# A state space stage whose decays get buffers of their own and whose four groups run as one strand

## The chip, the cores and the metric

The kernel runs on one core of a Trainium2 chip. The metric is device time in microseconds of one execution. The engines are named as the profile names them: PE (matmul; PEld its weight loads), DVE, ACT, POOL, and SP, whose queue issues the DMAs.

## The reference

A diffusion backbone of two layers over 256 latent and 256 context tokens, model width 1024. Each layer projects the normalised tokens once, for a state space mixer that runs in both directions, a differential attention and two gates, merges both branches, and ends in a gated feed-forward part. The change lies in the mixer: 16 heads of 64 in 4 groups, state 128, chunks of 128 tokens.

```python
def ssd_scan(xs, dt, a_head, b_mat, c_mat, h0):
    xd = (xs * dt[..., None]).reshape(bsz, nc, SSD_CHUNK, g, r, p)
    a = (dt * a_head).reshape(bsz, nc, SSD_CHUNK, g, r).transpose(0, 3, 4, 1, 2)
    a_cs = jnp.cumsum(a, axis=-1)
    ...
    cb = jnp.einsum('bclgn,bcsgn->bgcls', cc, bc)
    decay_in = jnp.exp(segsum(a))
    y_diag = jnp.einsum('bgcls,bgrcls,bcsgrp->bclgrp', cb, decay_in, xd)
    ...
    states = jnp.einsum('bclgn,bgrcl,bclgrp->bcgrpn', bc, decay_to_end, xd)
    ...
    y_off = jnp.einsum('bclgn,bcgrpn,bgrcl->bclgrp', cc, h_in, jnp.exp(a_cs))
    y = (y_diag + y_off).reshape(bsz, n, n_heads, p)
```

It is done for latent and context tokens, forward and on flipped sequences, and both results are added. The last layer needs the mixer's output for latent tokens alone.

## The kernel before

Everything lies with channels on partitions and tokens along the free dimension, in tiles of 128 tokens: four in layer 0 (`NT = 4`), two in layer 1. Each large product takes its weight from a list, `plan`: a DMA of 512 KB into `raw` (L304, on SP), a cast to the high part `whi` on ACT (L313), the low part `wlo` on DVE (L314), and then three matmuls per block of weight (L407 to L409). Products write PSUM banks; those of tag "mm" are two in number, those of tag "s", for small results, three.

The state space stage of a layer runs through four groups `g`. For each, a product gives two `xs` tiles, which `xbc_evac` takes out of PSUM by a convolution over tokens: `chv` on ACT (L568), two steps on DVE (L571, L572), a tanh `cth` (L665) and `xs` on DVE (L666). Then two generators are queued in two `lanes`: `states(g)` in lane 0 and `outputs(g)` in lane 1. A product calls `pump()` after each block of its weight, which lets the first generator of either lane go on to its next `yield`. So the program order of the mixer's instructions is woven into that of the large products by the number of `yield`s; a scheduler then orders each engine's queue, and keeps the matmuls of `pmm` and `ptr` in program order. A third queue, `trickle`, advanced by `drip()`, reads modulation weights (`mraw`, L463) and multiplies them (`pmmod`, L465).

`states(g)` transposes `xs` into `xT` (L910) and BF into `bT` (L916), and does six steps of the state: `xd = xT * ddt` on POOL (L925), a matmul into `psstate`, and `h` on ACT (L933) or DVE (L935, L938). It sets `sh["done"]`.

`outputs(g)` does, tile by tile:
- `fetch(t)` (L952): a DMA on SP's queue that spreads a row of cumulated decays over 128 partitions into `cs`, both directions and four heads, 512 KB. The tag `cs` has two buffers.
- `head(t)`: the matmul `cb` and its masked copy `cbm` (L961, DVE); `cc = exp(cs)` (L966, ACT); one subtraction for each direction, in place, on POOL (L969); the minimum of the two directions (L972, DVE), written into the first half of `cs`; its exponential `E` into the second half (L974, ACT); `cc` times CF (L975, DVE).
- X: for each of four heads a copy on ACT (L991) and a step on DVE (L992), then X times `E` (L993, DVE).
- the matmuls `pyyd` of X with `xT` and of `cc` with the states `h`, which wait for `sh["done"]`; after the last tile `xs` is updated from the result (L1014).

```python
            raw = fetch(0)
            yield 1
            nxt = head(0, raw)
            if NT > 1:
                raw = fetch(1)
            yield 1
            for t in range(NT):
                ...
                if t + 1 < NT:
                    nxt = head(t + 1, raw)
                    yield 1
                if t + 2 < NT:
                    raw = fetch(t + 2)
```

Of the kernel before, what the change touches and what calls it, by code (L numbers as in the profile page):

```python
# [10 lines left out]
F32 = mybir.dt.float32  # L11
F32R = mybir.dt.float32r
AF = mybir.ActivationFunctionType
ALU = mybir.AluOpType
AX = mybir.AxisListType

P = 128
D = 1024
# [41 lines left out]
def hybrid_backbone_kernel(  # L60
# [7 lines left out]
    V, A, G, T = nc.vector, nc.scalar, nc.gpsimd, nc.tensor  # L68
# [7 lines left out]
    def nm(s):  # L76
        cnt[0] += 1
        return f"{s}_{cnt[0]}"

    def bank(tag, what=""):  # L80
        return psp.tile([P, 512], F32, tag=tag, name=nm("p" + tag + what), bufs={"mm": 2, "s": 3, "y": 2, "m": 1}[tag])
# [246 lines left out]
    lanes = ([], [])  # L328
# [246 lines left out]
    for i in range(DEPTH):  # L575
        if i:
            L = col[i]
            m = L["mod"]
        full = i < DEPTH - 1
        NT = 4 if full else 2  # L580
        N = NT * P
# [359 lines left out]
                yield 1  # L941
            sh["done"] = True

        def outputs(g, sh):
            while "xT" not in sh:
                yield None
            xT, h_in = sh["xT"], sh["h"]
            yb = [bank("y", "yd"), bank("y", "yd")]

            def fetch(t):  # L950
                cs = up.tile([P, 2, 4, P], F32, tag="cs", name=nm("cs"), bufs=2)
                nc.sync.dma_start(cs.rearrange("p d h l -> p d (h l)"),  # L952
                                  csd[t, :, 4 * g:4 * g + 4, :].rearrange("d h l -> d (h l)").partition_broadcast(P))
                return cs

            def head(t, cs):
                tsl = slice(t * P, (t + 1) * P)
                cb = bank("s", "cb")
                pmm(cb[:, 0:P], BF[g][:, tsl], CF[g][:, tsl], start=True, stop=True)
                cbm = up.tile([P, 2, P], F32, tag="cbm", name=nm("cbm"), bufs=2)  # L960
                V.tensor_tensor(cbm, cb[:, 0:P].unsqueeze(1).to_broadcast([P, 2, P]), tri2, op=ALU.mult)  # L961

                cc = up.tile([P, 2, 4, P], F32, tag="cc", name=nm("cc"), bufs=2)
                dirs = [dr for dr in range(2) if not (dr == 0 and t == 2) and not (dr == 1 and t == 3)]
                d0, d1 = dirs[0], dirs[-1] + 1
                A.activation(cc[:, d0:d1], cs[:, d0:d1], AF.Exp)  # L966

                for dr in range(2):
                    G.tensor_tensor(cs[:, dr], cs[:, dr],  # L969
                                    csc[:, t, 16 * dr + 4 * g:16 * dr + 4 * g + 4].unsqueeze(2).to_broadcast([P, 4, P]),  # L970
                                    op=ALU.subtract)
                V.tensor_tensor(cs[:, 0], cs[:, 0], cs[:, 1], op=ALU.min)  # L972
                E = cs[:, 1]
                A.activation(E, cs[:, 0], AF.Exp)  # L974
                V.tensor_tensor(cc[:, d0:d1].rearrange("p d h l -> p (d h) l"), cc[:, d0:d1].rearrange("p d h l -> p (d h) l"),  # L975
                                CF[g][:, tsl].unsqueeze(1).to_broadcast([P, 4 * (d1 - d0), P]), op=ALU.mult)
                return cbm, cc, E, dirs

            raw = fetch(0)
            yield 1  # L980
            nxt = head(0, raw)
            if NT > 1:
                raw = fetch(1)
            yield 1
            for t in range(NT):
                tsl = slice(t * P, (t + 1) * P)
                cbm, cc, E, dirs = nxt
                X = up.tile([P, 4, P], F32, tag="X", name=nm("X"), bufs=2)
# [3 lines left out]
                    V.scalar_tensor_tensor(X[:, h, :], cbm[:, 1, :], dcol[1], X[:, h, :], op0=ALU.mult, op1=ALU.add)  # L992
                V.tensor_tensor(X, X, E, op=ALU.mult)  # L993
                yield 1
                if t + 1 < NT:
                    nxt = head(t + 1, raw)
                    yield 1
                if t + 2 < NT:
                    raw = fetch(t + 2)
                while "done" not in sh:  # L1000
                    yield None
                for f in range(2):
                    for h in (2 * f, 2 * f + 1):
                        r = slice(64 * (h % 2), 64 * (h % 2) + 64)
                        pmm(yb[f][r, tsl], xT[:, t, h * 64:(h + 1) * 64], X[:, h, :], start=True, stop=False)
                    for dr in dirs:
                        for h in (2 * f, 2 * f + 1):
                            r = slice(64 * (h % 2), 64 * (h % 2) + 64)
                            pmm(yb[f][r, tsl], h_in[dr, t][:, h * 64:(h + 1) * 64], cc[:, dr, h, :],
                                start=False, stop=dr == dirs[-1])  # L1010
                yield 1
            for f in range(2):
                j = 2 * g + f
                V.scalar_tensor_tensor(xs[j][:, 0:N], xs[j][:, 0:N], L["D"][:, j:j + 1], yb[f][:, 0:N],  # L1014
                                       op0=ALU.mult, op1=ALU.add)
            done.append(g)
            yield 1

        for g in range(4):
            for f, o in enumerate(gemm_f(hh, hl, 512, KD)):  # L1020
                xbc_evac(o, 512, xs[2 * g + f], 2 * g + f)
            sh = {}
            lanes[0].append(states(g, sh))
            lanes[1].append(outputs(g, sh))

        def gate_s(p):
            for f, o in enumerate(gemm_f(hh, hl, N, KD)):
# [179 lines left out]
```

## Time and profile before

| | us |
|---|---|
| median of 3 runs | 1745.26 (1743.87 to 1746.32) |
| the profiled execution's own time | 1740.01 |
| its span | 1738.2, mean granted clock of PE 0.993 |
| PE, DVE, ACT, POOL busy | 1667.1, 1148.0, 848.2, 181.3 |

The stage of layer 0 lies from about 405 to 580 us of the span, that of layer 1 from about 1346 to 1480. Rows of the profile are read like this. A group of the page is: line, engine, operation, result <- operands, shape, xcount | busy us, mean ns of one | idle us of the engine just before, and what ended it. A group of DMAs ends in its size and the us from issue to landing. A row of the timeline is: start us, us from first start to last end, engine, line, operation, xcount, and in brackets the idle time before it and what released it. A row of waits is: what waited for what, us in total, times, longest. A row of a window is: the stretch, its length, busy us of each engine (and instructions), the clock that PE was granted (1.00 is 2.4 GHz, 0.50 is 1.2 GHz), the DMA engines' busy share and GB/s.

### The profile page before, as it was taken

How to read it: one execution, taken by the hardware profiler on the slowest of the kernel's cores; microseconds unless marked ns; L12 is line 12 of the kernel's file. 1: busy time of each engine (PE TensorE's matmuls, PEld its weight loads, DVE VectorE, ACT ScalarE, POOL GpSimd, SP SyncE). 2: the span in 40 equal slices, each digit the busy share in tenths (PEclk: the TensorE clock that was granted, in tenths of full speed). 3: DMA queues.
4: the chain of work that ended last, by engine and by line, in shares of the span. 5: the costliest groups of instructions: out<-in, count | busy, mean ns of one | idle time of the engine just before them, and what ended most of it. 6: DMA issues, size and time to landing. Idle time of an engine off the chain costs nothing. (4 is left out here: it accounts for less than half of the span.)

```text
span 1738.2 us, 27022 instructions
## 1 busy us (share of the span) xinstructions
PE 1667.1 (96%) x10547; PEld 1406.2 (81%) x10547; DVE 1148.0 (66%) x2008; ACT 848.2 (49%) x1567; POOL 181.3 (10%) x212
## 2 busy tenths in 40 slices
PE   7999999999988999999999999999999898989997
PEld 4788878777766788888888888788879788989997
DVE  4776667325988855766666326666675789779964
ACT  3565665413545423644444225555655455466653
POOL 3000010001433000300000002100000252010000
PEclk9999999999999999999999999999999999989999
DMA  9644333555443234233323335844535445646653
GB/s 317 215 127 126 115 119 108 166 173 146 121 107 100 74 109 146 74 97 97 97 87 95 92 108 161 255 146 146 152 93 171 121 110 144 199 154 185 193 176 117
DMA packets 233199, 240.71 MB, mean 138 GB/s; under 512 B 10908, under 2 KB 223551, under 8 KB 233071
## 3 DMA queue, kind: packets, MB, share of 16 engines
q1 hardware_dynamic: 230720, 237.14, 45.4%
q8 instruction: 83, 1.36, 0.3%
q0 software_dynamic: 1312, 1.03, 0.2%
q10 hardware_dynamic: 1039, 0.81, 0.1%
q14 instruction: 45, 0.37, 0.1%
HBM read 234.62 MB, written 4.33 MB: 137 GB/s over the span
## 5 line engine op out<-in xcount | busy, mean ns | idle before, releaser
L314 DVE TENSOR_TENSOR wlo<-raw,whi 128x1024 fp32r<-128x1024 f32 (+1 forms) x318 | 388.3, 1221 | 255.7 <-ACT whi L313 254.8
L313 ACT CAST whi<-raw 128x1024 fp32r<-128x1024 f32 (+1 forms) x318 | 329.2, 1036 | 378.4 <-PE pmmmm L408 146.6
L407 PE MATMUL pmmmm<-th,whi 128*128 128x512 f32 x744 | 306.3, 412 | 1.6 <-DVE chv L572 1.6
L408 PE MATMUL pmmmm<-tl,whi 128*128 128x512 f32 x744 | 296.5, 399 | 0.0
L409 PE MATMUL pmmmm<-th,wlo 128*128 128x512 f32 x744 | 295.6, 397 | 0.0
L407 PEld LDWEIGHTS pmmmm<-th,whi 128*128 128x128 f32 x744 | 140.5, 189 | 42.2 <-issue 7.9
L409 PEld LDWEIGHTS pmmmm<-th,wlo 128*128 128x128 f32 x744 | 140.4, 189 | 34.5 <-issue 1.0
L408 PEld LDWEIGHTS pmmmm<-tl,whi 128*128 128x128 f32 x744 | 140.5, 189 | 31.0 <-issue 2.2
L393 PE MATMUL pmmmm<-th,whi 128*128 128x256 f32 x480 | 138.5, 289 | 1.5 <-ACT whi L313 1.3
L395 PE MATMUL pmmmm<-th,wlo 128*128 128x256 f32 x480 | 134.7, 281 | 0.6 <-DVE wlo L314 0.6
L394 PE MATMUL pmmmm<-tl,whi 128*128 128x256 f32 x480 | 134.8, 281 | 0.0
L969 POOL TENSOR_TENSOR cs<-cs,csc 128x512 f32<-128x512 f32 x48 | 69.1, 1454 | 264.0 <-DMA cs<-csd 141.5
L393 PEld LDWEIGHTS pmmmm<-th,whi 128*128 128x128 f32 x480 | 90.7, 189 | 6.2 <-issue 3.8
L394 PEld LDWEIGHTS pmmmm<-tl,whi 128*128 128x128 f32 x480 | 90.8, 189 | 0.7 <-issue 0.4
L395 PEld LDWEIGHTS pmmmm<-th,wlo 128*128 128x128 f32 x480 | 90.6, 189 | 0.8 <-DVE wlo L314 0.8
L409 PE MATMUL psmm<-th,wlo 128*128 128x512 f32 x200 | 79.3, 397 | 0.0
L725 ACT ACTIVATE e<-psscore,nmx 128x512 f32<-128x512 f32 (+1 forms) x96 | 58.1, 610 | 43.5 <-DVE nmx L722 40.5
L408 PE MATMUL psmm<-tl,whi 128*128 128x512 f32 x200 | 79.2, 396 | 0.0
L521 POOL TENSOR_TENSOR rs<-ms,mhalf 128x2 f32<-128x2 f32 x9 | 6.3, 699 | 698.5 <-DVE ms L518 698.5
L407 PE MATMUL psmm<-th,whi 128*128 128x512 f32 x200 | 79.0, 395 | 0.0
L722 DVE TENSOR_REDUCE nmx<-psscore 128x1 f32<-128x512 f32 (+1 forms) x80 | 51.8, 684 | 34.3 <-PE psscore L85 34.2
L441 PE MATMUL pmmmm<-whi,th 128*128 128x256 f32 x256 | 74.3, 290 | 0.0
(346 smaller groups left out, 3899.0 us busy)
## 6 DMA issues: line engine op xcount, KB each, us to landing
raw<-in_w_in_dram SPq DMA_DIRECT2D x124, 512.0 KB, 4.0
raw<-in_w_up_dram SPq DMA_DIRECT2D x88, 512.0 KB, 3.6
mraw<-in_w_mod_dram SPq DMA_DIRECT2D x80, 512.0 KB, 4.7
raw<-in_w_down_dram SPq DMA_DIRECT2D x45, 512.0 KB, 3.6
cs<-csd SPq DMA_DIRECT2D x24, 512.0 KB, 5.8
boot<-in_w_mod_dram SPq DMA_DIRECT2D x16, 512.0 KB, 9.3
raw<-in_w_br_att_dram SPq DMA_DIRECT2D x16, 512.0 KB, 3.6
raw<-in_w_br_ssd_dram SPq DMA_DIRECT2D x16, 512.0 KB, 3.5
```

The source lines that it names most:

```text
L313: pin(A.copy(hi[:, 0:n, :], raw[:, 0:n, :]))
L314: pin(V.tensor_tensor(lo[:, 0:n, :], raw[:, 0:n, :], hi[:, 0:n, :].bitcast(F32), op=ALU.subtract))
L393: T.matmul(o[f], whi[:, kk, cs], xh, start=first, stop=False)
L394: T.matmul(o[f], whi[:, kk, cs], xl, start=False, stop=False)
L395: T.matmul(o[f], wlo[:, kk, cs], xh, start=False, stop=last)
L407: T.matmul(o, whi[:, k % 4, cs], hi[k][:, 0:n], start=k == 0, stop=False)
L408: T.matmul(o, whi[:, k % 4, cs], lo[k][:, 0:n], start=False, stop=False)
L409: T.matmul(o, wlo[:, k % 4, cs], hi[k][:, 0:n], start=False, stop=k == k_tiles - 1)
L441: T.matmul(b[:, n, :], hi[k][:, ts], whi[:, k % 4, :], start=k == 0 and n == 0, stop=False)
L722: V.tensor_reduce(nmx[:, cc, 0:ng], sc[cc].rearrange("p (g k) -> p g k", g=ng), axis=AX.X, op=ALU.max, negate=True)
L725: A.activation(e[cc][:, g * w:(g + 1) * w], sc[cc][:, g * w:(g + 1) * w], AF.Exp, bias=nmx[:, cc, g:g + 1], accum_out=sm[:, cc, g:g + 1])
L969: G.tensor_tensor(cs[:, dr], cs[:, dr], csc[:, t, 16 * dr + 4 * g:16 * dr + 4 * g + 4].unsqueeze(2).to_broadcast([P, 4, P]), op=ALU.subtract)
```

## The change

Three things, all in `outputs`:
- The minimum is written into a tile of its own, `E` (two buffers), and its exponential is taken in place there; `cs` is read for the last time by that minimum.
- The four generators `outputs(g)` become one, over 4 x NT items (group, tile). It is queued before group 0's product; heads and X of an item need neither `xs` nor the states, and what waits for `done` of the item's group are the matmuls of y alone. The `yield` after the head and the one before it become one; the one after a group's update of `xs` joins that of the last tile.
- Two fetches are issued at the start, a third after the first head, and item n + 3's after the head of item n + 1. `cs` keeps two buffers.

```diff
@@ -941,19 +941,19 @@
                 yield 1
             sh["done"] = True
 
-        def outputs(g, sh):
-            while "xT" not in sh:
-                yield None
-            xT, h_in = sh["xT"], sh["h"]
-            yb = [bank("y", "yd"), bank("y", "yd")]
-
-            def fetch(t):
+        shs = []
+
+        def outputs():
+
+            items = [(g, t) for g in range(4) for t in range(NT)]
+
+            def fetch(g, t):
                 cs = up.tile([P, 2, 4, P], F32, tag="cs", name=nm("cs"), bufs=2)
                 nc.sync.dma_start(cs.rearrange("p d h l -> p d (h l)"),
                                   csd[t, :, 4 * g:4 * g + 4, :].rearrange("d h l -> d (h l)").partition_broadcast(P))
                 return cs
 
-            def head(t, cs):
+            def head(g, t, cs):
                 tsl = slice(t * P, (t + 1) * P)
                 cb = bank("s", "cb")
                 pmm(cb[:, 0:P], BF[g][:, tsl], CF[g][:, tsl], start=True, stop=True)
@@ -969,20 +969,19 @@
                     G.tensor_tensor(cs[:, dr], cs[:, dr],
                                     csc[:, t, 16 * dr + 4 * g:16 * dr + 4 * g + 4].unsqueeze(2).to_broadcast([P, 4, P]),
                                     op=ALU.subtract)
-                V.tensor_tensor(cs[:, 0], cs[:, 0], cs[:, 1], op=ALU.min)
-                E = cs[:, 1]
-                A.activation(E, cs[:, 0], AF.Exp)
+                E = up.tile([P, 4, P], F32, tag="E", name=nm("E"), bufs=2)
+                V.tensor_tensor(E, cs[:, 0], cs[:, 1], op=ALU.min)
+                A.activation(E, E, AF.Exp)
                 V.tensor_tensor(cc[:, d0:d1].rearrange("p d h l -> p (d h) l"), cc[:, d0:d1].rearrange("p d h l -> p (d h) l"),
                                 CF[g][:, tsl].unsqueeze(1).to_broadcast([P, 4 * (d1 - d0), P]), op=ALU.mult)
                 return cbm, cc, E, dirs
 
-            raw = fetch(0)
+            coming = [fetch(*items[0]), fetch(*items[1])]
             yield 1
-            nxt = head(0, raw)
-            if NT > 1:
-                raw = fetch(1)
+            nxt = head(*items[0], coming.pop(0))
+            coming.append(fetch(*items[2]))
             yield 1
-            for t in range(NT):
+            for n, (g, t) in enumerate(items):
                 tsl = slice(t * P, (t + 1) * P)
                 cbm, cc, E, dirs = nxt
                 X = up.tile([P, 4, P], F32, tag="X", name=nm("X"), bufs=2)
@@ -992,13 +991,16 @@
                     V.scalar_tensor_tensor(X[:, h, :], cbm[:, 1, :], dcol[1], X[:, h, :], op0=ALU.mult, op1=ALU.add)
                 V.tensor_tensor(X, X, E, op=ALU.mult)
                 yield 1
-                if t + 1 < NT:
-                    nxt = head(t + 1, raw)
-                    yield 1
-                if t + 2 < NT:
-                    raw = fetch(t + 2)
-                while "done" not in sh:
+                if n + 1 < len(items):
+                    nxt = head(*items[n + 1], coming.pop(0))
+                if n + 3 < len(items):
+                    coming.append(fetch(*items[n + 3]))
+                yield 1
+                while len(shs) <= g or "done" not in shs[g]:
                     yield None
+                if t == 0:
+                    yb = [bank("y", "yd"), bank("y", "yd")]
+                xT, h_in = shs[g]["xT"], shs[g]["h"]
                 for f in range(2):
                     for h in (2 * f, 2 * f + 1):
                         r = slice(64 * (h % 2), 64 * (h % 2) + 64)
@@ -1008,20 +1010,21 @@
                             r = slice(64 * (h % 2), 64 * (h % 2) + 64)
                             pmm(yb[f][r, tsl], h_in[dr, t][:, h * 64:(h + 1) * 64], cc[:, dr, h, :],
                                 start=False, stop=dr == dirs[-1])
-                yield 1
-            for f in range(2):
-                j = 2 * g + f
-                V.scalar_tensor_tensor(xs[j][:, 0:N], xs[j][:, 0:N], L["D"][:, j:j + 1], yb[f][:, 0:N],
-                                       op0=ALU.mult, op1=ALU.add)
-            done.append(g)
-            yield 1
-
+                if t == NT - 1:
+                    for f in range(2):
+                        j = 2 * g + f
+                        V.scalar_tensor_tensor(xs[j][:, 0:N], xs[j][:, 0:N], L["D"][:, j:j + 1], yb[f][:, 0:N],
+                                               op0=ALU.mult, op1=ALU.add)
+                    done.append(g)
+                yield 1
+
+        lanes[1].append(outputs())
         for g in range(4):
             for f, o in enumerate(gemm_f(hh, hl, 512, KD)):
                 xbc_evac(o, 512, xs[2 * g + f], 2 * g + f)
             sh = {}
+            shs.append(sh)
             lanes[0].append(states(g, sh))
-            lanes[1].append(outputs(g, sh))
 
         def gate_s(p):
             for f, o in enumerate(gemm_f(hh, hl, N, KD)):
```

**DVE at the start of layer 0's state space stage.** `pmmmm` is the bank of the first product, `wlo` the low part of a weight. Before:

```order
L314 TENSOR_TENSOR wlo_3910<-raw_3889,whi_3909 128x1024 [waits DMAHW3_49,Activation_49]
L571 SCALAR_TENSOR_TENSOR chv_3939<-pmmmm_3913,cols_157,chv_3939 128x2x255 [waits Activation_49]
L572 SCALAR_TENSOR_TENSOR chv_3939<-pmmmm_3913,cols_157,chv_3939 128x2x255 [waits DVE_49]
L666 SCALAR_TENSOR_TENSOR xs_0_3874<-cth_3938,chv_3939 128x512 [waits Activation_49]
L314 TENSOR_TENSOR wlo_3980<-raw_3895,whi_3979 128x1024 [waits DMAHW5_49,PE_49,Activation_49]
L975 TENSOR_TENSOR cc_4060<-cc_4060,CF_0_617 128x1024 [waits Activation_49]
L972 TENSOR_TENSOR cs_4044<-cs_4044 128x512 [waits DMAHW3_49,Pool_49]
L571 SCALAR_TENSOR_TENSOR chv_3971<-pmmmm_3945,cols_157,chv_3971 128x2x255 [waits Activation_49]
```

DVE there in the changed kernel:

```order
L314 TENSOR_TENSOR wlo_3910<-raw_3889,whi_3909 128x1024 [waits DMAHW3_49,Activation_49]
L961 TENSOR_TENSOR cbm_3932<-pscb_3930,kt 128x256 [waits PE_49]
L975 TENSOR_TENSOR cc_3934<-cc_3934,CF_0_617 128x1024 [waits Activation_49]
L973 TENSOR_TENSOR E_3938<-cs_3920 128x512 [waits DMAHW0_49,Pool_49]
L991 SCALAR_TENSOR_TENSOR X_3950<-cbm_3932,dtT_621,X_3950 128x128 [waits Activation_49] x4
L961 TENSOR_TENSOR cbm_3968<-pscb_3966,kt 128x256 [waits PE_49]
L992 TENSOR_TENSOR X_3950<-X_3950,E_3938 128x512 [waits DVE_49,Activation_49]
L973 TENSOR_TENSOR E_3974<-cs_3922 128x512 [waits DMAHW1_49,Pool_49]
L975 TENSOR_TENSOR cc_3970<-cc_3970,CF_0_617 128x1024
L571 SCALAR_TENSOR_TENSOR chv_3981<-pmmmm_3913,cols_157,chv_3981 128x2x255 [waits Activation_49]
L314 TENSOR_TENSOR wlo_4022<-raw_3895,whi_4021 128x1024 [waits DMAHW5_49,PE_49,Activation_49]
L572 SCALAR_TENSOR_TENSOR chv_3981<-pmmmm_3913,cols_157,chv_3981 128x2x255 [waits DVE_49]
```

The heads of tiles 0 and 1 and the X of tile 0 now stand before L571 and L572, which empty the first product's bank. (In the changed kernel the minimum is L973, X's step on DVE L991 and its product with E L992.)

**SP at the same place**, from the fetch of the weights for that product's successors on. Before:

```order
L304 DMA raw_3977<-in_w_in_dram 128x4x256 [waits DMAHW1_49,DVE_49]
L463 DMA mraw_3985<-in_w_mod_dram 128x4x256 [waits DMAHW4_49,PE_49]
L304 DMA raw_3983<-in_w_in_dram 128x4x256 [waits DMAHW3_49,DVE_49]
L463 DMA mraw_3991<-in_w_mod_dram 128x4x256 [waits DMAHW6_49,PE_49]
L952 DMA cs_4044<-csd_623 128x2x512 [waits DMASW5_49,DMASW4_49,Pool_49]
L952 DMA cs_4067<-csd_623 128x2x512 [waits DMASW7_49,DMASW6_49]
L304 DMA raw_4144<-in_w_in_dram 128x4x256 [waits DMAHW5_49,DVE_49]
L304 DMA raw_4150<-in_w_in_dram 128x4x256 [waits DMAHW7_49,DVE_49]
L952 DMA cs_4124<-csd_623 128x2x512 [waits DMASW1_49,DMASW0_49,DMAHW3_49,DVE_49,Activation_49]
```

SP there in the changed kernel:

```order
L304 DMA raw_4019<-in_w_in_dram 128x4x256 [waits DMAHW1_49,DVE_49]
L952 DMA cs_3920<-csd_623 128x2x512 [waits DMASW4_49,DMASW5_49,PE_49,Pool_49]
L952 DMA cs_3922<-csd_623 128x2x512 [waits DMASW7_49,DMASW6_49]
L304 DMA raw_4025<-in_w_in_dram 128x4x256 [waits DMAHW3_49,DVE_49]
L463 DMA mraw_4027<-in_w_mod_dram 128x4x256 [waits DMAHW4_49,PE_49]
L952 DMA cs_3942<-csd_623 128x2x512 [waits DMASW1_49,DMASW0_49,DMAHW0_49,DVE_49,Activation_49]
L463 DMA mraw_4033<-in_w_mod_dram 128x4x256 [waits DMAHW6_49,DMAHW5_49,PE_49]
L952 DMA cs_3978<-csd_623 128x2x512 [waits DMASW3_49,DMASW2_49,DMAHW1_49,DVE_49,Activation_49]
L304 DMA raw_4146<-in_w_in_dram 128x4x256 [waits DMAHW7_49,DVE_49]
```

The first two `cs` fetches moved ahead of a `raw` and two `mraw`; the third stands before the second `mraw` and waits for DVE's minimum, among others.

**POOL in group 2 of layer 0.** `xd` feeds the state's matmuls. Before, tiles 0, 1 and 2 are `cs_4790`, `cs_4814`, `cs_4883`:

```order
L969 TENSOR_TENSOR cs_4790<-cs_4790,csc_622 128x512 [waits DMAHW5_49,DVE_49,Activation_49]
L969 TENSOR_TENSOR cs_4790<-cs_4790,csc_622 128x512
L925 TENSOR_TENSOR xd_4786<-xT_4566,ddt_624 128x256 [waits PE_49]
L969 TENSOR_TENSOR cs_4814<-cs_4814,csc_622 128x512 [waits DMAHW6_49,DVE_49,Activation_49]
L969 TENSOR_TENSOR cs_4814<-cs_4814,csc_622 128x512
L925 TENSOR_TENSOR xd_4836<-xT_4566,ddt_624 128x256 [waits PE_49]
L969 TENSOR_TENSOR cs_4883<-cs_4883,csc_622 128x512 [waits DMAHW1_49,DVE_49]
L969 TENSOR_TENSOR cs_4883<-cs_4883,csc_622 128x512 [waits Activation_49]
```

POOL there in the changed kernel, where tiles 0 to 3 are `cs_4644`, `cs_4722`, `cs_4783`, `cs_4847`:

```order
L969 TENSOR_TENSOR cs_4644<-cs_4644,csc_622 128x512 [waits DMAHW4_49,DVE_49,Activation_49]
L969 TENSOR_TENSOR cs_4644<-cs_4644,csc_622 128x512
L925 TENSOR_TENSOR xd_4812<-xT_4574,ddt_624 128x256 [waits PE_49]
L925 TENSOR_TENSOR xd_4869<-xT_4574,ddt_624 128x256 [waits PE_49]
L969 TENSOR_TENSOR cs_4783<-cs_4783,csc_622 128x512 [waits DMAHW7_49,DVE_49]
L969 TENSOR_TENSOR cs_4722<-cs_4722,csc_622 128x512 [waits DMAHW6_49,Activation_49]
L969 TENSOR_TENSOR cs_4722<-cs_4722,csc_622 128x512
L969 TENSOR_TENSOR cs_4847<-cs_4847,csc_622 128x512 [waits DMAHW0_49,DVE_49]
L969 TENSOR_TENSOR cs_4783<-cs_4783,csc_622 128x512 [waits Activation_49]
```

The first subtraction of tile 2 now stands ahead of both of tile 1, and the first of tile 3 ahead of the second of tile 2.

## Rows read from the trace of the kernel before

**Rows 1.** the page, busy time of each engine:

```profile
PE 1667.1 (96%) x10547; PEld 1406.2 (81%) x10547; DVE 1148.0 (66%) x2008; ACT 848.2 (49%) x1567; POOL 181.3 (10%) x212
```

**Rows 2.** windows of the state space stages (columns above):

```profile
430.00:578.00 148.00, 133.19 (x814) 104.56 (x813) 126.78 (x226) 74.20 (x152) 53.63 (x50) 0.98 0.41 103
516.00:518.00 2.00, 2.00 (x10) 1.38 (x11) 1.83 (x5) 0.10 (x1) 0.00 (x0) 0.50 0.63 143
530.00:532.00 2.00, 2.00 (x12) 1.44 (x9) 1.97 (x5) 1.72 (x3) 0.35 (x2) 0.55 0.00 0
1365.00:1367.00 2.00, 2.00 (x6) 1.52 (x5) 2.00 (x4) 0.14 (x1) 0.00 (x0) 0.50 0.85 264
```

**Rows 3.** waits of PE, 415 to 600 us:

```profile
PE pyyd L85 <- DVE X L993: 8.2, 7, 2.1
PE psstate L85 <- POOL xd L925: 6.5, 4, 3.4
PE psssT L88 <- DVE xs L666: 2.1, 1, 2.1
```

**Rows 4.** waits of DVE, 430 to 578 us:

```profile
DVE cc L975 <- ACT cc L966: 8.1, 5, 2.7
DVE cs L972 <- POOL cs L969: 6.8, 6, 1.6
```

**Rows 5.** waits of POOL, 430 to 578 us:

```profile
POOL cs L969 <- DMA cs<-csd: 29.2, 5, 9.9
```

**Rows 6.** waits of SP's DMA queue, 400 to 600 us:

```profile
SPq L952 <- DVE X L993: 66.5, 11, 10.3
```

**Rows 7.** timeline around the two longest gaps, first PE, then POOL:

```profile
513.13 0.70 PE L85 MATMUL psstate<-xd,bT 128*128 128x256 f32 x2 [3.41 <-POOL xd L925]
...
527.48 0.70 PE L85 MATMUL psstate<-xd,bT 128*128 128x256 f32 x2 [2.63 <-POOL xd L925]
...
508.26 4.06 POOL L969 TENSOR_TENSOR cs<-cs,csc 128x512 f32<-128x512 f32 x2 [2.30 <-ACT cc L966]
512.28 0.79 POOL L925 TENSOR_TENSOR xd<-xT,ddt 128x256 f32<-128x256 f32 x1
```

**Rows 8.** timeline of DVE, layer 0, and last a row of ACT:

```profile
414.29 0.75 DVE L572 SCALAR_TENSOR_TENSOR chv<-pmmmm,cols,chv 128x510 f32<-128x510 f32 x1
...
417.88 2.06 DVE L975 TENSOR_TENSOR cc<-cc,CF 128x1024 f32<-128x1024 f32 x1
...
426.75 1.21 DVE L975 TENSOR_TENSOR cc<-cc,CF 128x1024 f32<-128x1024 f32 x1
...
515.34 1.13 DVE L992 SCALAR_TENSOR_TENSOR X<-cbm,dtT,X 128x128 f32<-128x128 f32 x4
516.50 0.69 DVE L993 TENSOR_TENSOR X<-X,cs 128x512 f32<-128x512 f32 x1
...
501.17 1.06 ACT L966 ACTIVATE cc<-cs 128x1024 f32<-128x1024 f32 x1 [2.51 <-DMA cs<-csd]
```

**Rows 9.** timeline at layer 0's start: PE, POOL, SP:

```profile
419.18 0.50 PE L407 MATMUL pmmmm<-th,whi 128*128 128x512 f32 x1
...
426.88 0.66 PE L88 MATMUL psssT<-kt,xs 128*128 128x128 f32 x4 [2.10 <-DVE xs L666]
...
417.79 5.50 POOL L969 TENSOR_TENSOR cs<-cs,csc 128x512 f32<-128x512 f32 x4 [112.32 <-DMA cs<-csd]
...
409.03 1.00 SPq L952 DMA_DIRECT2D cs<-csd  x2
```

**Rows 10.** timeline of PE at the start of layer 1's stage:

```profile
1359.37 0.47 PE L407 MATMUL pmmmm<-th,whi 128*128 128x512 f32 x1 [1.58 <-DVE chv L572]
...
1363.96 0.63 PE L88 MATMUL psssT<-kt,xs 128*128 128x128 f32 x4 [2.94 <-DVE xs L666]
```

**Rows 11.** the page, a group of instructions and one of DMAs:

```profile
L314 DVE TENSOR_TENSOR wlo<-raw,whi 128x1024 fp32r<-128x1024 f32 (+1 forms) x318 | 388.3, 1221 | 255.7 <-ACT whi L313 254.8
...
cs<-csd SPq DMA_DIRECT2D x24, 512.0 KB, 5.8
```

## The prediction

> **What bounds the kernel now.** The engine table comes first: PE is busy 96% of the span, so time is lost or won only where PE waits or runs at the low clock [rows 1]. Next the stages. In layer 0's state space stage (430 to 578 us) PE is busy for 133.19 of 148 us, and DVE for 126.78, 86% [rows 2]: this is one of the few places where PE has gaps, 14.8 us of them, and DVE has few. What ends PE's gaps is in the waits between 415 and 600: 8.2 us for X after its product with the decays, in 7 waits, 6.5 us for `xd` of POOL in 4 waits, and 2.1 us for `xs` of DVE [rows 3].
>
> Behind them stands the decay chain. DVE waits 8.1 us for the exponential `cc` of ACT and 6.8 for the subtractions on `cs` of POOL [rows 4]; POOL waits 29.2 us for the DMA of `cs` [rows 5]; and SP's queue, which issues that DMA, waits 66.5 us in 11 waits for L993, X times the decays [rows 6]. That last wait is the buffer: the decays lie in half of `cs`, so `cs` is free only after L993.
>
> The two longest gaps show how it reaches PE. At 512.28 POOL makes the `xd` which PE starts on at 513.13, 3.41 us late; ahead of it POOL did two subtractions, 4.06 us from 508.26 [rows 7]. At 527.48 the same, 2.63 us late [rows 7]. Right after both, PE runs at a granted clock of 0.50 and 0.55, its 1.2 GHz level, instead of 1.00 [rows 2]; so does it after the 2.94 us gap at 1363.96 in layer 1 [rows 2, 10]. Each dip lasts about 3.4 us, an estimate from the three windows of two us at that level, each the middle of a dip, and half the clock over it costs 1.7 us; I book this for each gap over 2.5 us, the shortest that shows it being 2.63.
>
> **The change part by part.** No arithmetic is added or taken away; the four edits move work and free a buffer.
>
> *E of its own.* `cs` comes free after the minimum L973 instead of after X times E. Between these stand four X instructions (1.13 us together) and the product itself, 0.69 [rows 8], with the exponential on ACT, some 0.6 as half of what `cc`'s takes for twice the elements, 1.06 [rows 8]: about 2.5 us earlier for each tile. The minimum writes as many elements as before: nothing.
>
> *Three ahead.* The text asks for tile n+3 right after the head of n+1, but there are still two `cs` buffers, so the issue waits for the minimum of that very head. Within a group this is little more than the 2.5 us; across the group's end it is new: the next group's first tiles are fetched before the old group ends, so that DVE's and POOL's work on them no longer piles up behind the landing of `cs`, as where ACT waits 2.51 us for it at 501.17 [rows 8]. Both gaps [rows 7] with their dips, 3.41 + 2.63 + 2 x 1.7 = 9.4 us, are booked as gone.
>
> What comes in their place is in POOL's order: in group 2 the first subtraction of tile 2 now stands ahead of both of tile 1, and tile 2's DMA starts only behind the minimum of tile 0. That chain is the issue and landing, 5.8 us [rows 11], three subtractions at 1.4 each (5.50 for four [rows 9]) and a minimum (0.69, as the product of the same width [rows 8]): 10.7. PE's work for a tile, 133.19 / 16 = 8.3 us [rows 2], covers the rest: 2.4 us of gap, with a dip 4.1 (a dip because DVE's `wlo`, 1.2 us [rows 11], is queued behind that minimum and the gap grows by it). Between its ends, no gap at all and twice this, 8.2, I take it once, as the order shows it that way at one group's middle. Gain 9.4 - 4.1 = 5.3.
>
> *One strand, heads ahead.* X of a group's first tiles is ready earlier. Of the 8.2 us of waits for X [rows 3] I book half, 4.1, as gone, and 1.0 back, since merged yields leave two advances less in a group between a head and its matmuls: gain 3.1. Ends: 0, as DVE is 86% busy and must do the work somewhere [rows 2], and 8.2.
>
> *The start of the stage, layer 0.* Here the change costs. Before, DVE does the evacuation of the first product (L571, L572, done at 414.29 + 0.75 = 415.0 [rows 8]) ahead of everything else, and the third product on PE, at 419.18 [rows 9], finds its bank free. Now head 0, X 0 and head 1 stand in front on DVE and ACT: `cs`, now on SP right behind a `raw` and ahead of two fetches that it followed, issued some 2.8 us earlier than at 409.03 [rows 9], at 406.2, and landed 5.8 us on [rows 11], at 412; exponential to 413.1, two subtractions to 415.9, minimum 416.6; the second pair to 418.7, its minimum 419.4; `cc` times CF, which takes 2.06 us beside POOL [rows 8], to 421.5; L571, `wlo`, L572 at 0.75, 1.2 and 0.75 to 424.2. The third product waits 5.0 us. It and the transposes beside it take 5.6 us (419.18 to 424.78, where the gap before 426.88 begins [rows 9]), so PE reaches the transposes of the second `xs` at 429.8. By then `xs` is ready, behind one more L571 to L666 chain, so the 2.10 us gap before 426.88 [rows 9] goes, and 5.0 - 2.1 = 2.9 are lost; some 0.7 of PE's other work (`mraw`'s matmuls) moves into the gap. That leaves 2.2, with a dip that was not there 3.9. Ends: 1, if the scheduler's order hides the exponential, and 7, if POOL's and DVE's instructions stretch each other throughout. In the same place `mraw`'s second half is queued on SP behind a `cs` fetch that waits for the minimum at 416.6; landing after about the 5.8 us of its neighbour [rows 11] at 422.4, it is late for its matmuls, which stand between the second product and the third, but inside the gap just booked: nothing by itself.
>
> *The start, layer 1.* There PE already has gaps of 1.58 us for L572 and 2.94 for `xs` [rows 10], since a head stands on DVE ahead of L572 before the change too. With X and the second head ahead as well, as the four X, the product, a minimum and `cc` times CF (1.13 + 0.69 + 0.69 + 2.06 [rows 8]) L572 ends some 4.6 later, the first gap grows to 6.2, and the second, 2.94, is covered: 6.2 - 1.58 - 2.94 = 1.7 lost, the dip staying one. Ends: -2 (the second gap's dip goes too) and +4 (the second gap stays).
>
> The rest of both layers keeps its instructions and its waits: nothing.
>
> DVE's second operand port bears on the start. The row shows L975 at 2.06 us while POOL subtracts (417.79 to 423.29) and at 1.21 alone [rows 8, 9]. The Trainium skill (SBUF — State Buffer, Who interferes with whom) says that GpSimd and a DVE instruction with two SBUF inputs exclude each other on one shared port pair. By the row alone the start costs 3.9 us; by a full exclusion, DVE's six two-input instructions there would wait for up to all four subtractions, 5.5 us, and the start would cost 7, which is an estimate by that page.
>
> **Sum.** 5.3 + 3.1 - 3.9 - 1.7 = 2.8 us gained. The profiled execution took 1740.01 us (span 1738.2), and would take 1737.2. The median of the runs, 1745.26, lies 5.25 above it, so I forecast 1742.5. What is under 0.2%, 3.5 us, a measurement of this kernel can't tell from no change: this is just inside.
>
> **The rivals.** *DVE sets the stage's end (faster).* If PE only follows DVE here, DVE's waits on the decay chain are what goes: 8.1 + 6.8 = 14.9 us [rows 4], less the starts' 5.6: 9.3 gained, 1736.0. For it: 86% of DVE against 14.8 us of gaps on PE [rows 2]. Against: PE's gaps name DVE's X and POOL's `xd`, not `wlo`, which feeds every product. The Trainium skill (Perfetto Trace Analysis, Identifying the Most-Contended Engine) judges DVE by its busy share and TensorE by that of its weight loads; these are 86% and 104.56 of 148, 71%, so by that page DVE is the engine that binds, and this rival's time is the one it gives.
>
> *The evacuation behind the heads (slower).* One mechanism at one place: L572 of the first product, on DVE, behind two heads whose `cs` must land first. If its end is at 429 instead of 424.2, as when the landing takes 3 us longer or the port doubles each of four instructions, 4.8 us more are lost in layer 0 and about half, 2.4, in layer 1, where a head was ahead of it already. With a gain of 6 left in the middle that is 6 - 5.6 - 7.2 = -6.8: 1752.1. At 1.5 us lost for each us of L572 the sum's 2.8 is gone from 2 us beyond 424.2 on, and a measurable loss begins at 4.2. For it: PE's gaps at both starts already wait for that chain [rows 3, 10].
>
> *It does not do what it says.* With two buffers the third fetch ahead is the second in time. If the early fetch across the group's end is undone by the same wait, only the 2.5 us of E remain, the gaps at 513 and 527 shrink to under 1 us each with their dips gone or halved, 4 to 5 us, and that meets the 5.6 of the starts: about 1746, no change.
>
> **How the numbers follow.** The sum's case, 0.36, most of it within 0.2% and its upper part faster; DVE as the bound, 0.25; the evacuation, 0.22; no effect, 0.17. From these: faster by over 0.2% 0.37 (0.25 and a third of the first), slower 0.24 (0.22 and a little of the last), within 0.2% 0.39. The range reaches from a little beyond the faster rival, the gap's lower end (4.1 less to pay) counted in half, 1734, to the slower rival, 1752.5.
>
> **What the profile of the changed kernel would show.** Right: SP's waits for L993 gone, in their place shorter ones for L973; no `xd` wait over 2.5 us in groups 2 and 3; a PE gap near 419 for `chv` L572 of about 5 us with the low clock behind it. Wrong: no gap near 419 (then the start was free, and the time lies near the faster rival), or POOL's waits for the DMA of `cs` still near 29 us (then the fetch was not early), or several gaps over 2.5 us between 440 and 560.

## The result and the profile after

The changed kernel takes 1752.87 us (median of 5 runs, 1750.91 to 1753.65) against 1745.26 before: 1.0041 times as long, 95% interval 1.0026 to 1.0055. The profiled executions are 1752.87 and 1740.01 us, spans 1751.1 and 1738.2. Their difference, 12.9 us, is more than that of the medians, 7.6, since the profiled execution of the kernel before was 5 us quicker than its median. So stretches that several kernels repeat count for more below than single totals. Each stretch is read from one profiled execution of its kernel.

To place the loss I cut both traces at the same pieces of PE's work: the matmuls `pmmod` of 16 at 405.80 (405.89 after), the transposes of BF of each group, and the first matmul of the gate's statistics (L493), which closes a layer's stage.

| stretch | before | after | difference |
|---|---|---|---|
| layer 0, start: `pmmod` to BF of group 0 | 21.58 | 26.58 | +5.00 |
| layer 0, middle: BF of group 0 to L493 | 164.77 | 163.98 | -0.79 |
| up to the last attention transposes of layer 1 | 721.46 | 721.51 | +0.05 |
| layer 1, start: from there to BF of group 0 | 56.99 | 59.42 | +2.43 |
| layer 1, groups: BF of group 0 to BF of group 3 | 80.05 | 81.65 | +1.60 |
| layer 1, tail: BF of group 3 to L493 | 28.27 | 31.76 | +3.49 |
| from there to the end | 259.28 | 260.31 | +1.03 |

First the waits of PE in layer 0's stage, 405 to 610 us, which answer to [rows 3]:

```profile
PE pmmmm L409 <- DVE wlo L314: 4.8, 1, 4.8
PE pyyd L85 <- DVE X L992: 4.7, 5, 2.1
PE pmmod L465 <- DMA mraw<-in_w_mod_dram: 4.4, 2, 4.1
PE psssT L88 <- DVE h L938: 2.1, 1, 2.1
PE pyyd L85 <- DVE h L938: 1.3, 1, 1.3
```

The waits for `xd`, 6.5 us, are gone and those for X are 4.7 in place of 8.2. What is new is 4.8 for `wlo`, 4.4 for `mraw` (at the start), and 3.4 for `h`. Over the whole middle, from BF of group 0 to L493, before and then after (columns as in [rows 2]):

```profile
427.40:592.20 164.80, 149.26 (x888) 116.98 (x886) 137.50 (x244) 80.71 (x163) 55.51 (x53) 0.98 0.40 103
432.50:596.50 164.00, 149.78 (x885) 117.35 (x883) 136.51 (x231) 78.96 (x155) 52.70 (x51) 0.97 0.36 97
```

PE stands idle there for 14.2 us in place of 15.5, at a mean clock of 0.97 in place of 0.98. Behind these waits are those of SP's queue (400 to 600), of POOL and of DVE (430 to 582), for [rows 4 to 6]:

```profile
SPq L952 <- DVE E L973: 75.6, 13, 11.1
...
POOL cs L969 <- DMA cs<-csd: 17.5, 3, 8.5
...
DVE E L973 <- POOL cs L969: 7.9, 6, 2.9
DVE cc L975 <- ACT cc L966: 3.6, 2, 2.2
```

The buffer's release moved from L993 to the minimum, as written, but SP's queue waits as long for it: 75.6 us after 66.5. POOL's wait for the DMA fell from 29.2 to 17.5, DVE's for `cc` from 8.1 to 3.6; DVE's for POOL rose from 6.8 to 7.9. And the granted clock, in three windows after the change and, last, the window of the kernel before that answers to the third:

```profile
420.00:430.00 10.00, 6.21 (x24) 4.40 (x25) 9.02 (x11) 4.44 (x7) 2.91 (x2) 0.66 0.72 226
1364.00:1374.00 10.00, 4.75 (x13) 3.89 (x14) 8.52 (x12) 4.71 (x8) 1.50 (x1) 0.52 0.71 191
1470.00:1480.00 10.00, 7.30 (x35) 5.23 (x35) 9.45 (x19) 3.06 (x8) 3.01 (x2) 0.69 0.19 53
...
1461.60:1471.60 10.00, 7.35 (x74) 5.86 (x73) 9.56 (x25) 3.18 (x8) 0.92 (x2) 1.00 0.01 2
```

**The start of layer 0**, PE, SP, POOL and DVE in the timeline:

```profile
419.09 0.64 PE L465 MATMUL pmmod<-mraw,s 128*32 128x256 f32 x8 [0.30 <-DMA mraw<-in_w_mod_dram]
423.79 1.08 PE L465 MATMUL pmmod<-mraw,s 128*32 128x256 f32 x8 [4.05 <-DMA mraw<-in_w_mod_dram]
...
416.70 0.37 SPq L952 DMA_DIRECT2D cs<-csd  x1
417.17 0.41 SPq L463 DMA_DIRECT2D mraw<-in_w_mod_dram  x1
...
412.87 3.03 POOL L969 TENSOR_TENSOR cs<-cs,csc 128x512 f32<-128x512 f32 x2 [107.30 <-ACT cc L966]
...
415.93 0.69 DVE L973 TENSOR_TENSOR E<-cs 128x512 f32<-128x512 f32 x1 [1.93 <-POOL cs L969]
...
419.83 0.68 DVE L973 TENSOR_TENSOR E<-cs 128x512 f32<-128x512 f32 x1
420.43 1.21 DVE L975 TENSOR_TENSOR cc<-cc,CF 128x1024 f32<-128x1024 f32 x1
...
423.36 0.73 DVE L572 SCALAR_TENSOR_TENSOR chv<-pmmmm,cols,chv 128x510 f32<-128x510 f32 x1
```

The minimum ends at 416.62 and the third `cs` fetch goes out at 416.70; only then does SP reach `mraw`, at 417.17, which has landed at 423.79. L572, which frees the bank for the third product, ends at 424.09. Two waits end within 0.3 us of each other, and the trace names the one of them that PE meets first.

**The middle of layer 0**, where PE waits longest (POOL, DVE, PE):

```profile
515.77 4.11 POOL L969 TENSOR_TENSOR cs<-cs,csc 128x512 f32<-128x512 f32 x3 [4.45 <-DMA cs<-csd]
...
519.92 0.69 DVE L973 TENSOR_TENSOR E<-cs 128x512 f32<-128x512 f32 x1 [2.93 <-POOL cs L969]
...
521.19 2.35 DVE L314 TENSOR_TENSOR wlo<-raw,whi 128x1024 fp32r<-128x1024 f32 x2
...
522.46 0.80 PE L409 MATMUL pmmmm<-th,wlo 128*128 128x512 f32 x1 [4.82 <-DVE wlo L314]
```

POOL's first subtraction on tile 2 waits 4.45 us for its DMA and holds up both of tile 1 behind it; DVE's minimum waits for those, `wlo` stands behind the minimum, and PE waits for `wlo`.

**Layer 1**, PE at the start (1369.25), in the groups (1433.44) and in the tail, for [rows 10]:

```profile
1369.25 0.77 PE L407 MATMUL pmmmm<-th,whi 128*128 128x512 f32 x1 [6.68 <-DVE chv L572]
...
1433.44 0.67 PE L85 MATMUL psstate<-xd,bT 128*128 128x256 f32 x2 [1.15 <-ACT bT L916]
...
1471.90 0.70 PE L85 MATMUL psstate<-xd,bT 128*128 128x256 f32 x2 [1.17 <-POOL xd L925]
...
1474.49 1.19 PE L85 MATMUL psstate<-xd,bT 128*128 128x256 f32 x2 [1.53 <-DVE h L938]
```

### The profile page after: what moved, and what is told of

It is laid out like the page before. It is cut to its first block, busy times and chain, and to the rows that moved or that the text cites. A ratio compares the mean times of both kernels' runs of the same rounds, so it can differ in the third digit from the quotient of the medians.

```text
span 1751.1 us, 27041 instructions
## 1 busy us (share of the span) xinstructions
PE 1674.7 (96%) x10547; PEld 1410.7 (81%) x10547; DVE 1153.6 (66%) x2008; ACT 849.7 (49%) x1567; POOL 180.2 (10%) x212
## 3 DMA queue, kind: packets, MB, share of 16 engines
q0 software_dynamic: 1312, 1.03, 0.3%
```

## The experiments

The theory after the result, S: the loss is made at the two starts. Its rival, M: it is made in the middle, by the order in which heads and state steps stand on DVE and POOL. The table gives each kernel's median, its ratio to the kernel before with the interval, and its stretches as differences to before, in us. A ratio compares with executions of the kernel before that were taken beside that run, whose medians lay between 1744.59 and 1746.06; so ratios are compared below, rather than medians of different rows. The long stretch between the layers is left out: it is 3.5 us longer in e3_noE, 2.0 in e8_gate, 1.8 in e4_third, and within 0.8 of before in the others. Chance has its part in these traces: the anchor of start 0, ahead of the work that the edits touch, lies anywhere from 405.3 to 410.1 us.

| run | median | ratio | start 0 | middle 0 | start 1 | groups 1 | tail 1 |
|---|---|---|---|---|---|---|---|
| the change | 1752.87 | 1.0041 (1.0026 to 1.0055) | +5.0 | -0.8 | +2.4 | +1.6 | +3.5 |
| e1_late | 1746.75 | 1.0017 (1.0001 to 1.0034) | +0.2 | -1.6 | -0.5 | +1.0 | +3.3 |
| e2_Eonly | 1741.52 | 0.9982 (0.9969 to 0.9994) | 0.0 | -1.2 | -1.2 | -0.1 | +1.5 |
| e3_noE | 1750.66 | 1.0039 (1.0024 to 1.0054) | +4.7 | -3.1 | +1.9 | +1.7 | +1.4 |
| e4_third | 1752.68 | 1.0047 (1.0030 to 1.0064) | +6.0 | -3.0 | +1.3 | +1.9 | +1.5 |
| e5_hold | 1747.17 | 1.0003 (0.9984 to 1.0022) | +2.1 | -2.3 | -1.4 | +1.7 | +1.4 |
| e6_bufs3 | 1744.17 | 0.9992 (0.9972 to 1.0011) | +1.2 | -4.5 | +0.4 | +1.1 | +3.3 |
| e8_gate | 1745.34 | 0.9996 (0.9977 to 1.0016) | 0.0 | -2.6 | 0.0 | +1.1 | +1.9 |
| e9_b3 | 1741.24 | 0.9979 (0.9965 to 0.9993) | +1.2 | -1.3 | +0.8 | 0.0 | +2.7 |
| e10_early | 1742.35 | 0.9989 (0.9977 to 1.0002) | 0.0 | -3.3 | +0.1 | -0.1 | +1.5 |
| e11_Eagain | 1742.19 | 0.9992 (0.9978 to 1.0005) | 0.0 | -2.3 | -1.2 | -0.1 | +1.5 |
| e12_nomul | 1740.96 | 0.9971 (0.9953 to 0.9989) | -0.7 | -1.3 | -1.3 | -1.3 | +2.0 |
| e13_b3early | 1742.83 | 0.9985 (0.9968 to 1.0003) | +1.6 | -4.8 | +1.2 | 0.0 | 0.0 |

**The strand queued later** (e1_late):

```diff
-        lanes[1].append(outputs())
         for g in range(4):
...
             lanes[0].append(states(g, sh))
+            if g == 0:
+                lanes[1].append(outputs())
```

> The change, with its one strand queued after group 0's product instead of before it, in both layers. Theory S (the loss is made at the two starts, where the heads stand ahead of the first product's evacuation and a cs fetch ahead of mraw's second half): the 5.1 us of layer 0's start and the 2.0 of layer 1's come back, 1752.9 - 7 = 1746 us, and the transposes of BF of group 0 lie within 1 us of where they lay before the change. Theory M (the loss is made in the middle, by the order in which heads and state steps stand on DVE and POOL): under 3 us come back, over 1750.

S, in the main: both starts are as before the change (+0.2, -0.5), and the time falls from 1.0041 to 1.0017 of the kernel before, some 4.2 us (6.1 between the medians). It stays at 1.0017, though: the rest is not in the starts.

**E alone** (e2_Eonly, and again as e11_Eagain): the kernel before with the three lines on `E` of the change's diff.

> The kernel before, with the minimum and its exponential in a tile E of their own, and nothing else of the change. Theory S: the buffer alone costs nothing and shortens the two longest waits for xd by 2.5 us each, so 0 to 5 us gained with a dip or two less: 1740 to 1745, and SP's waits for X times E turn into shorter ones for the minimum. Theory M: the buffer's earlier release itself disturbs the order: 1747 or more. The forecast's booking of 9.4 us for those waits would be 1736.

> The kernel before with E alone, a second time, beside the next two on one chip. If the 0.18% gained the first time is E's: 0.997 to 0.999 of the kernel before, again. If it was the spread of the executions: 0.999 to 1.001.

The first time as S has it, 1741.52 us or 0.9982, and less than the 9.4 us of the forecast. The second time, 0.9992, falls where the spread of the executions had been expected (0.999 to 1.001), and its interval reaches 1. So that E alone costs nothing is shown; that it gains is not. In its first trace PE's waits for `xd` are down from 6.5 to 3.5 us, those for X up from 8.2 to 8.8, and SP's waits for the minimum, expected to be shorter than those for L993 had been, are as long: 66.8 us for 66.5.

**The strand without E** (e3_noE): the minimum in `cs` again, the rest of the change kept.

> The change with the minimum written into cs again, so that a fetch waits for X times E as before; strand and three fetches ahead stay. Theory S: the starts are as in the change, and the fetches of the middle are 2.5 us later: 1753 to 1757. If E is worth nothing inside the strand, as theory M has it: 1752 to 1754.

Within the strand E is worth nothing that can be measured, 1.0039 for 1.0041, and the time lies below both ranges. In its trace PE waits 5.3 us for `wlo` where the change waits 4.8, and the middle is 2.3 us shorter all the same.

**The third fetch behind `mraw`** (e4_third), **and the heads held with the fetches early** (e5_hold). These separate the two waits at layer 0's start.

```diff
             nxt = head(*items[0], coming.pop(0))
-            coming.append(fetch(*items[2]))
             yield 1
...
-                if n + 3 < len(items):
+                if 0 < n and n + 3 < len(items):
                     coming.append(fetch(*items[n + 3]))
                 yield 1
+                if n == 0:
+                    for _ in range(4):
+                        yield 1
+                    coming += [fetch(*items[2]), fetch(*items[3])]
```

> The change, with the third and the fourth fetch asked for four steps later, so that they stand behind mraw's second half on SP; heads stay ahead of the first product's evacuation. If both waits end together, as 423.8 for mraw and 424.1 for L572 in the change's trace say, the gap stays and only changes its name to chv L572, about 4.5 us: 1752 to 1753. If mraw alone makes the gap: 4 to 5 us back, 1748, and no wait for chv over 1 us.

```diff
             coming = [fetch(*items[0]), fetch(*items[1])]
             yield 1
+            while not shs:
+                yield None
```

> The change, with the strand queued before group 0's product as it is, so that the first two cs fetches go out early, but with the first head held until that product is through. Theory S: only the heads' place and the third fetch behind them make the loss at the starts, so BF's transposes of group 0 come within 1 us of the kernel before in layer 0 and 1 us earlier or the same in layer 1; 1745 to 1747, as when the whole strand is queued later. If the early cs fetches themselves cost (they stand on SP ahead of a raw and two mraw): 2 us or more are lost up to BF of group 0, 1749.

PE's rows at that place, first of e4_third:

```profile
422.46 0.64 PE L465 MATMUL pmmod<-mraw,s 128*32 128x256 f32 x8 [0.72 <-DMA mraw<-in_w_mod_dram]
423.93 0.64 PE L465 MATMUL pmmod<-mraw,s 128*32 128x256 f32 x8 [0.82 <-DMA mraw<-in_w_mod_dram]
428.25 0.76 PE L407 MATMUL pmmmm<-th,whi 128*128 128x512 f32 x1 [3.69 <-DVE chv L572]
```

then of e5_hold:

```profile
422.78 0.64 PE L465 MATMUL pmmod<-mraw,s 128*32 128x256 f32 x8 [1.57 <-DMA mraw<-in_w_mod_dram]
424.23 1.08 PE L465 MATMUL pmmod<-mraw,s 128*32 128x256 f32 x8 [0.81 <-DMA mraw<-in_w_mod_dram]
425.24 0.80 PE L407 MATMUL pmmmm<-th,whi 128*128 128x512 f32 x1
```

With `mraw` moved ahead the gap changes its name to `chv` and the start stays 6.0 us longer; with the heads held, and SP's order still against `mraw`, 2.1 are left, which is what the second case of e5_hold had for layer 0. So the heads ahead of the evacuation make the gap, and the queue on SP, which the change's trace names and which costs 2.1 us alone, is hidden behind it. In layer 1, where no `mraw` is fetched there, the change's start is 2.4 longer, and with the heads held it is 1.4 shorter than before.

**A third `cs` buffer in the strand** (e6_bufs3: the strand queued later, `bufs=3` for `cs`, minimum in `cs`):

> The strand queued after group 0's product, with three cs buffers, and with the minimum written into cs again, since E and a third cs don't fit together. Theory: the wait of about 5 us for wlo near 522 in layer 0 comes from a fetch that can't start before a minimum while POOL's next instruction waits for it; with a third buffer the fetch is three ahead in time too, the wait is under 1 us, and 5 + 1.7 us come back: 1740. Rival: DVE and ACT are late themselves, and the wait stays over 3 us: 1745 to 1748.

POOL and PE at the place of the wait for `wlo`:

```profile
506.78 1.04 POOL L969 TENSOR_TENSOR cs<-cs,csc 128x512 f32<-128x512 f32 x1 [1.49 <-DMA cs<-csd]
...
515.82 0.80 PE L409 MATMUL pmmmm<-th,wlo 128*128 128x512 f32 x1 [3.74 <-DVE wlo L314]
```

POOL's wait for the DMA falls from 4.45 to 1.49 us, PE's for `wlo` only from 4.82 (5.39 in e1_late) to 3.74: by that number the rival's case. The time, 1744.17, lies between the two. 2.9 us of middle come back against e1_late.

**Heads held to their group** (e8_gate): the strand queued later, and

```diff
-                if n + 1 < len(items):
+                if t + 1 < NT:
                     nxt = head(*items[n + 1], coming.pop(0))
...
+                if t == NT - 1 and n + 1 < len(items):
+                    while len(shs) <= g + 1 or "xT" not in shs[g + 1]:
+                        yield None
+                    nxt = head(*items[n + 1], coming.pop(0))
+                    yield 1
```

(the first head likewise waits for `xT`).

> The strand queued after group 0's product, with heads of a group held until its xT is there, as before the change; E and the fetches ahead across a group's end stay. If it is the heads ahead of a group's state steps that cost in the middle (the waits of layer 1 for xd and bT, 0.8 us a group and the longer end): layer 1's stage is as with E alone, and the whole 1739 to 1742. If the fetches ahead on SP cost, it stays at 1745 to 1747.

The time, 1745.34, is the second case's, the waits are neither's. Those for `wlo` and for `bT` are gone, but in layer 0 PE waits 6.1 us for X and, where [rows 3] has none, 4.2 for `h`; and layer 1's groups still lose 1.1.

**Buffers and fetches without a strand** (e9_b3: the kernel before with `bufs=3` for `cs`; e10_early: E, and `fetch(0)`, `fetch(1)` at the start of each group's generator, ahead of the wait for `xT`; e13_b3early: both, without E):

> The kernel before with three cs buffers in place of two, and nothing of the change. If what E gives is the earlier fetch, a third buffer gives it too, and earlier: SP's waits for X times E go, and 0.997 to 0.999. If E's gain is another (one read fewer of cs, the order on DVE): 1.000.

> The kernel before with E, each group's first two fetches asked for at the start of its generator, ahead of the wait for xT; heads stay where they were. If the fetch across the group's end was worth its 5 us in the middle and only the heads ahead spoil it: 0.996 to 0.998, and less than with E alone. If the fetch ahead collides with raw on SP, or is worth nothing once E is there: 0.998 to 1.001.

> The kernel before with three cs buffers and each group's first two fetches at the start of its generator; minimum in cs, no strand. If both pieces add: 0.996 to 0.997 of the kernel before. If the third buffer gives all there is: 0.997 to 0.999.

One constant, three buffers, gives 0.9979, with an interval below 1. Its trace has the same mark as that of E alone: PE's waits for `xd` are 3.6 us and those for X 7.8.

```profile
PE pyyd L85 <- DVE X L993: 8.8, 6, 3.9
PE psstate L85 <- POOL xd L925: 3.5, 3, 2.3
...
PE pyyd L85 <- DVE X L993: 7.8, 6, 3.9
PE psstate L85 <- POOL xd L925: 3.6, 3, 2.4
```

(405 to 610 us, e2_Eonly and then e9_b3.) That both gain by the buffer's earlier release fits this, but isn't shown: SP's waits for L993, which were to go, are 67.8 us in 10 waits, and the trace of e9_b3, an execution of 1747.60 us, well above its median, is shorter than before only in the middle, by 1.3. The early fetch adds nothing that these intervals can tell.

**DVE relieved** (e12_nomul): the strand queued later, without L975.

> The strand queued after group 0's product, with the product of cc and CF (L975, DVE, 24 instructions, about 28 us in both layers) left out of the computation. If DVE's own work and not the fetches made the middle give nothing back: PE's gaps between BF's transposes of group 0 and the statistics of layer 0 (163.2 us with the product in) shrink by 6 us or more, the wait of 5 us for wlo goes under 2, and the whole is 1734 to 1738. If the fetch and its landing set the pace: the stretch keeps 161 us or more, and the whole 1743 to 1746.

Neither case: the stretch keeps its length as the second has it, 163.5 us, but the time lies below that case's range. From 425 to 588 us DVE is busy for 127.80 us, against 142.58 in as long a window of e1_late (second row), and the wait for `wlo` is gone: from BF of group 1 to L493 6.0 us come back. But the whole middle is as long as in e1_late, 163.5 us against 163.2, as BF of group 0 to that of group 1 takes 6.3 more:

```profile
425.00:588.00 163.00, 148.45 (x881) 117.13 (x880) 127.80 (x228) 81.89 (x164) 53.19 (x53) 0.97 0.40 101
427.00:590.00 163.00, 146.23 (x876) 114.71 (x875) 142.58 (x243) 82.49 (x164) 55.34 (x53) 0.98 0.40 102
...
434.95 1.04 POOL L969 TENSOR_TENSOR cs<-cs,csc 128x512 f32<-128x512 f32 x1 [2.53 <-DMA cs<-csd]
...
436.62 1.22 PE L85 MATMUL psstate<-xd,bT 128*128 128x256 f32 x2 [3.84 <-POOL xd L925]
```

`xd` now stands behind a subtraction that waits for a DMA: a gap like the old ones of [rows 7], at another place. So in this stretch DVE's total does not set the length. That the order does, by what stands behind a wait, is how the rows read; no run shows it by itself. Layer 1 is another matter: there 0.7 us at the start, 2.4 in the groups and 1.3 in the tail did come back against e1_late (PE's waits in the groups fall from 2.8 us to 0.6), and the whole kernel went from 1.0017 to 0.9971. There the product that was left out had its price.

## Why the prediction was wrong

Forecast 1742.5, measured 1752.87, 0.4 us beyond the range.

*The starts: right, somewhat too small.* Booked 3.9 + 1.7; the trace has 5.0 + 2.4, and e1_late gives them back. The chain held: minimum forecast for 416.6, ended 416.62; L572 for 424.2, ended 424.09; layer 1's gap for 6.2, 6.68. The tenth of L572 is luck, since two errors cancelled: the second minimum ended at 420.51 and not at 419.4, and L975 behind it took 1.21 us and not 2.06. That `mraw` costs nothing by itself inside that gap nearly held in the change, where the third product began at 424.80, 0.7 after L572; alone, SP's order costs 2.1 (e5_hold). Mis-sized were the clock's dips: after the 6.68 us gap the clock of 1364 to 1374 is 0.52, where 1.7 us had been booked as the dip staying one.

*The middle of layer 0: the failed step.* "Both gaps with their dips ... are booked as gone" held, and so did the wait in their place, down to POOL's first subtraction of tile 2. Its size did not: 2.4 us booked, 4.82 measured. And "I take it once" left out a wait for `h` before the transposes, 2.11 us, with low clock behind it (0.50 from 488 to 490), though it is shorter than the 2.5 us from which a dip had been booked. X's waits fell by 3.5, and 1.3 came back at `h`, against a booked gain of 3.1. The clock took back what the waits gave: behind the 4.82 us gap it is 0.50 from 522 to 528, where one dip of 1.7 had been booked. Of 8.4 us booked, 0.8 came. One reading was wrong too, that the gap at 527.48 was made as the one at 513.13: POOL's two subtractions were done by 525.40 there, and `xd` waited for `xT` of DVE, which stood behind the minimum on the same late `cs`.

```profile
522.92 2.48 POOL L969 TENSOR_TENSOR cs<-cs,csc 128x512 f32<-128x512 f32 x2 [9.85 <-DMA cs<-csd]
526.82 1.72 POOL L925 TENSOR_TENSOR xd<-xT,ddt 128x256 f32<-128x256 f32 x2 [1.41 <-DVE xT L910]
```

The runs show how a sum of this kind fails here: with E or without, with the heads ahead or held, with two buffers or three, with 14.8 us less on DVE, the middle stays within 5 us of 164.77. In the traces each order removes one wait and makes another; taking one off the list was not worth its length. Why just these waits appear, and not others, stays open.

*"The rest of both layers keeps its instructions and its waits: nothing": the second failed step.* Layer 1's groups lose 1.6 and its tail 3.5. The groups' 1.0 to 1.9 is in every kernel with the one strand except e12_nomul, and in none without; the wait for `bT` on ACT (1433.44 above) is part of it in the change. The tail's 3.5 is the clock, 0.69 over ten microseconds where it was 1.00: PE's waits in the tail come to 4.6 us after and 4.4 before. The tail takes 28.3 us in two of the fourteen traces, 29.6 to 30.9 in nine and 31.6 to 31.8 in three (the change, e1_late, e6_bufs3). In e3_noE the same waits for `xd` and `h`, 2.5 and 1.5 us, are not followed by low clock (1.00 from 1461 to 1491). So the tail's loss looks like chance in part, and with one trace of each kernel that isn't settled.

*The rivals.* The slower one had the sign and the place, but its price rested on L572 ending at 429, and it ended at 424.1. In the traces 7.6 us of booked gain are missing in the middle, 5.1 are lost in the rest of layer 1, and 1.8 more than booked at the starts; that its 1752.1 is so near is luck. DVE as the bound fell, for layer 0's middle, with e12_nomul, where 14.8 us less of DVE left the stretch as long; in layer 1 leaving that product out did pay. By the Trainium skill (Perfetto Trace Analysis, Identifying the Most-Contended Engine) DVE's 86% would name it; in layer 0's middle the measurement decides against that. "It does not do what it says" was half right: with two buffers SP waits 75.6 us for the release, where its waits were to be shorter than the 66.5 before, and in the strand E is worth nothing (e3_noE).

One statement ahead of the prediction was loose: within a tile the strand has as many `yield`s as before; the two fewer of a group are at its start and end.

The kernel before gains 0.2% from a third `cs` buffer (0.9979, one run, its interval below 1); with E alone (0.9982 and 0.9992) the second interval reaches 1.

## What to carry to other kernels

Before work is queued ahead of a stage, look at what stands in front of the bank or buffer that the next product needs: here two heads delayed one evacuation on DVE, and a queue on SP hid behind the same gap. Where two waits end together, undo each alone, since the trace names one. To fetch further ahead, add the buffer first: three loose fetches over two buffers left SP's queue waiting for the release as long as before (75.6 us after 66.5). And a wait that is taken off the list is not yet time gained: look for the one that stands behind it.

## What was not expected

The low clock lasted longer than the 3.4 us that the kernel before showed (514 to 520 at 0.68, 0.50 and 0.97): of 5 windows of two us from 518 to 528 in e1_late, around the end of a gap of 5.39, four show it (0.84, 0.50, 0.50, 0.50). It begins inside the gap there, which ends at 521.55, and costs PE nothing until then. After the 6.68 us gap of layer 1, which ends at 1369.25, it holds until 1374. And DVE beside POOL is not always the one that is slowed: L975 took 2.06 us beside the subtractions before [rows 8, 9], and 1.23 at 412.77 after, while POOL's two, 1.04 each where one runs alone (506.78 in e6_bufs3), took 3.03 together:

```profile
412.77 1.23 DVE L975 TENSOR_TENSOR cc<-cc,CF 128x1024 f32<-128x1024 f32 x1 [2.14 <-ACT cc L966]
```

In the first L975 began 0.09 us behind POOL, in the second 0.10 ahead of it. By the Trainium skill (SBUF — State Buffer, Who interferes with whom) the shared port pair is an exclusive lock. The two rows agree with one engine waiting for the other, and show that it may be either.
